# A hybrid decoder layer on one core: first weights on ScalarE's queue, and last additions ahead of the preceding scalings

## The chip, the core and the metric

The kernel runs on one core of a Trainium2 chip. A core has five engines with an instruction queue each. TensorE (PE in the profile) multiplies matrices; PEld is its loading of the stationary operand. VectorE (DVE) and ScalarE (ACT) work on tiles elementwise, GpSimd (POOL) too, and SyncE (SP) mostly issues DMAs. A DMA is an instruction on the queue of the engine that issues it, and its data are moved by 16 DMA engines that all queues share. An engine executes its queue in order, and an instruction that waits for a semaphore holds up everything behind it.

The metric is the device time of one execution, in microseconds (us). Less is better.

## The reference, cut to what matters

One pre-norm layer: a root-mean-square norm of 16 meta tokens and 512 tokens of width 2048, one combined input projection, three causal token mixers on its columns, a gate on each branch, one output projection with a residual add, and a final norm.

```python
def hybrid_layer(x, norm_w, w_in, ...):
    h = rms_norm(x, norm_w)
    ...
    proj = (h @ w_in).astype(f32)
    (dq, dk, dv, dz, db, da, gq, gk, gv, gz, gl, fq, fk, fv, fz, ff) = split_cols(proj)
    ...
    o_dn = gated_head_norm(o_dn, dz, ...)          # gated delta rule, 6 heads
    o_gla = gated_head_norm(o_gla, gz, ...)        # gated linear attention, 5 heads
    o_fox = o_fox.reshape(fz.shape) * jax.nn.silu(fz)   # forgetting attention, 5 heads
    o = jnp.concatenate([o_dn, o_gla, o_fox], axis=-1)
    return x + o @ w_out

def reference(x, meta_tokens, ...):
    h = jnp.concatenate([meta, x], axis=1)
    h = hybrid_layer(h, ...)
    return rms_norm(h, final_norm_w)[:, N_META:]
```

All of it is float32. The kernel keeps that accuracy on TensorE by writing each operand as a sum of two parts, hi and lo, and adding three products: hi by hi, hi by lo, and lo by hi.

## The kernel before

**Scheduling.** The program is written with a tile framework. A scheduler orders each engine's queue with a simulated timeline of its own, by priorities and by the dependencies that it is given. The kernel adds dependencies that cost no semaphore ("NoSync": they only fix an order on one engine); `paced`, `behind` and `ring` are such. DMAs from SP and ACT take one of eight completion semaphores in turn (order shows them as DMAHW0 to DMAHW7), and a DMA that takes a semaphore again waits until the DMA that held it before has landed.

**The start.** The norm's weight is folded into the transposed input. For a 128-row block k of the width, `load_x` makes `xh{k}` (ACT, scaled copy of the raw block `xs`, line 302) and `xl{k}` (DVE, the rest, line 303). Two blocks come in one tile: `xs0` holds blocks 0 and 1, and is loaded as two DMAs (line 287); `xs1` to `xs7` are one DMA each (line 280). Tokens are scaled by their norm only after the projection, so a second copy of the input in token order, `xt00` to `xt41` (line 349, 512 KB each for tokens, less for meta tokens), is squared and summed on ACT (line 350).

The first four column blocks of the projection (gates `dz` of heads 0 to 3, `NF = 4`) are computed together, because their four sums can use the same input blocks as they come. Their weights come in quarters of the depth: `raw{i}q{q}` is quarter q of weight i, 256 KB (line 186). A weight is split by `split`: `pace[0]` is ACT's copy to hi (line 170), `pace[1]` DVE's subtraction that gives lo (line 171). A quarter of depth has 4 blocks, 4 weights and 3 products, 48 matmuls of 512 columns (line 314, sums `pp0`, `pp1`, `pp2`, `pp12` in the order of the queue). While TensorE waits for the first data, it multiplies a tile of ones, ten times (`warm`, line 309), and once more behind the first three real matmuls (line 335).

Other loads of the start are 8 KB of constants on ACT's queue (`cpk`, columns 0 to 15, line 126: the norm weight that `xh` and `xl` need), the remaining 42.5 KB of constants (line 136) and a mask `lm` (line 137), which `more_constants` reads on DVE as `dnws` and `lmk` (lines 139 and 138).

**The middle.** Every other block of the input projection follows with 1024-column loads, split in the same way; the mixers' smaller work is placed between their matmuls. The output projection uses sums and differences of weight blocks that GpSimd's accumulating DMAs build. None of it is touched.

**The end.** The output is computed for four token blocks `tb` of 128 and four column groups `cc` of 512. For the last group, `cc` 3, TensorE finishes the token blocks one after the other (`pt30`, `pt31`, `pt32`, `pt33` with 384 columns, and `pz` with the last 128). For each token block DVE adds TensorE's sum to the accumulator that holds the residual (`add`, line 1429, tiles `acc` and `accs`), ACT squares and sums (`square`, line 1436), DVE makes the mean (lines 1601 and 1602; 1597 and 1598 for the last block), ACT takes logarithm and exponential to get the reciprocal root `r` (lines 1608 and 1609), and the four groups are scaled by it: groups 0 and 2 on ACT (line 1613), group 1 on DVE (line 1617), group 3 on DVE together with the final norm's weight (line 1615). Each group then goes out by DMA (line 1618). For the last token block the 384 columns are squared on ACT and the last 128 by one DVE instruction (line 1605). GpSimd multiplies groups 0 to 2 by the final norm's weight beforehand (`weigh`, line 1439).

Of the kernel before, what the change touches and what calls it, by code (L numbers as in the profile page):

```python
# [8 lines left out]
F32 = mybir.dt.float32  # L9
F32R = mybir.dt.float32r  # L10
# [3 lines left out]
AF = mybir.ActivationFunctionType  # L14
ALU = mybir.AluOpType
# [3 lines left out]
P = 128  # L19
D = 2048  # L20
# [6 lines left out]
EPS = 1e-6  # L27
# [15 lines left out]
def _cols():  # L43

    def run(start, n):
        return list(range(start, start + n))

    none = lambda n: [-1] * n
    gates = run(5004, 16) + run(5004, 16) + run(3072, 6) + run(3078, 6) + run(7580, 5) + none(15)
    blocks, name = [], {}  # L50

    def add(key, cols):
        name[key] = len(blocks)
        blocks.append(cols)

    for g in range(2):
        for h in range(H * g, H * g + H):
            add(("dz", h), run(2304 + P * h, P))
        for what, start in (("dk", 768), ("dv", 1536), ("dq", 0)):
            for h in range(H * g, H * g + H):  # L60
                add((what, h), run(start + P * h, P))
    for h in range(GLA_HEADS):
        add(("gz", h), run(4364 + P * h, P))
    for p in range(3):
        if p < 2:
            add(("gk", p), run(3404 + P * p, P))
            add(("gq", p), run(3084 + P * p, P))
        else:
            add(("gk", p), run(3404 + P * p, 64) + run(3084 + P * p, 64))
        for h in range(2 * p, min(2 * p + 2, GLA_HEADS)):  # L70
            add(("gv", h), run(3724 + P * h, P))
    for h in range(FOX_HEADS):
        for what, start in (("fk", 5660), ("fv", 6300), ("fq", 5020), ("fz", 6940)):
            add((what, h), run(start + P * h, P))
    return gates, [c for b in blocks for c in b], name


GATE_COLS, COLS, BLOCK_OF = _cols()
# [4 lines left out]
def tile_hybrid_trunk(ctx, tc, xT, xtok, mtok, w_gate, w_in, w_out, w_dn, consts, lmask, fin_w, out, dbg=None):  # L83
    nc = tc.nc
# [6 lines left out]
    six = pool("six", 14)  # L91
# [5 lines left out]
    def row(name, dt=F32):  # L97
        return wk.tile([P, 3 + T], dt, tag="row", bufs=7, name=name)
# [4 lines left out]
    V, A, G, PE = nc.vector, nc.scalar, nc.gpsimd, nc.tensor  # L103
# [20 lines left out]
    nwc, cwc = cpk[:, 0:16], cpk[:, 16:88].rearrange("p (b w) -> p b w", w=4)  # L124
# [43 lines left out]
    def split(raw, hi, lo):  # L168
        with tc.high_priority(offset=1000000):
            pace[0] = A.copy(hi, raw).ins  # L170
            pace[1] = V.tensor_tensor(out=lo, in0=raw, in1=hi.bitcast(F32), op=ALU.subtract).ins  # L171
            splits.append(pace[1])
            heads_.append(pace[0])
# [3 lines left out]
    def paced(*ins):  # L177

        for x in ins:
            tc.add_manual_dep(x.ins, pace[x.ins.engine == pace[1].engine].name, mybir.DependencyInfo(  # L180
                mybir.DependencyClass.NoSync, mybir.DependencyReason.DATA), reason="paced")

    def raw_rows(src, name):

        raw = row(f"raw{name}")[:, : src.shape[-1]]
        nc.sync.dma_start(out=raw, in_=src)
        return raw, name

    def split_rows(raw, name):

        n = raw.shape[-1]
        both = six.tile([P, 2, 512], F32R, tag="six", name=f"w{name}")
        hi, lo = both[:, 0, :n], both[:, 1, :n]
        split(raw, hi, lo)
        return hi, lo


    def part(name, n=512):
        return hp.tile([P, T], F32R, tag="x", name=name)[:, :n]
# [37 lines left out]
    xh, xl = [], []  # L237
# [32 lines left out]
    NF = 4  # L270

    def first_quarter(i, q):
        return raw_rows(w_in[BLOCK_OF["dz", i], q // 2][:, (q % 2) * 512 : (q % 2 + 1) * 512], f"{i}q{q}")

    xs = {}

    def fetch_x(c):
        xs[c] = six.tile([P, 2, T], F32, tag="six", name=f"xs{c}")
        if c > 0:
            nc.sync.dma_start(out=xs[c], in_=xT[:, 2 * c : 2 * c + 2, :])  # L280

    firsts = []

    def fetch_first():
        fetch_x(0)
        for j in range(2):
            nc.sync.dma_start(out=xs[0][:, j], in_=xT[:, j])
            firsts.append(first_quarter(j, 0))
        firsts.extend(first_quarter(i, 0) for i in (2, 3))
        fetch_x(1)  # L290

    def load_x(c):
        if c not in xs:
            fetch_x(c)
        t = xs[c]
        for j in range(2):
            k = 2 * c + j
            if c == 0 and j == 1:
                wq.append(split_rows(*firsts[0]))
            xh.append(part(f"xh{k}", T))  # L300
            xl.append(part(f"xl{k}", T))
            A.activation(xh[k], t[:, j], AF.Copy, scale=nwc[:, k : k + 1])
            V.scalar_tensor_tensor(out=xl[k], in0=t[:, j], scalar=nwc[:, k : k + 1],
                                   in1=xh[k].bitcast(F32), op0=ALU.mult, op1=ALU.subtract)


    pw = psm.tile([P, 512], F32, tag="m", name="warm")
# [12 lines left out]
    for q in range(4):  # L320
        wq = []
# [22 lines left out]
    for b in range(5):  # L344
        r = NM if b == 4 else P
        for c in range(2):
            t = wp.tile([P, 1024], F32, tag=("raw", "hi", "lo")[(2 * b + c) % 3], name=f"xt{b}{c}")
            src = mtok if b == 4 else xtok[b * P : (b + 1) * P]
# [6 lines left out]
    for b in range(5):  # L355
        r = NM if b == 4 else P
# [85 lines left out]
    raw = row("rawgk")[:48, :320]  # L442
# [193 lines left out]
    raw = {}  # L636
# [771 lines left out]
    def mms(p_, o, w, s, first, last):  # L1408
        for n, (o_, w_) in enumerate(((o[0], w[0]), (o[0], w[1]), (o[1], w[0]))):
            mm = PE.matmul(p_, o_[:, s], w_, start=(first and n == 0), stop=(last and n == 2), skip_group_check=True)  # L1410
            order.append(mm.ins)
# [15 lines left out]
    def add(tb, cc, p_, c=slice(0, 512), op=ALU.add):  # L1427
        a = acc[tb, cc][:, c]
        return V.tensor_tensor(out=a, in0=a, in1=p_[:, c], op=op)
# [4 lines left out]
    def square(tb, cc, c=slice(0, 512), n=0):  # L1434
        sq = row(f"sqf{tb}{cc}{n}")
        A.activation(sq[:, c], acc[tb, cc][:, c], AF.Square, accum_out=ss[:, tb, cc + n : cc + n + 1])

    def weigh(tb, cc):
        return G.tensor_tensor(out=acc[tb, cc], in0=acc[tb, cc], in1=fw[cc], op=ALU.mult)  # L1439
# [45 lines left out]
    for j in pairs:  # L1485
        r = raw[j]
        paced(V.scalar_tensor_tensor(out=r["a12"], in0=r["a12"], scalar=-1.0, in1=r["s2"], op0=ALU.mult,
                                     op1=ALU.subtract))
        r["s4"] = r["a12"]
    for mm, n in later:  # L1490
        n = head[n[0]] + n[1] if isinstance(n, tuple) else n
# [66 lines left out]
    fw, marks = [], []  # L1558
    for c in range(4):
        f = part(f"fw{c}").bitcast(F32)  # L1560
# [16 lines left out]
    for cc in range(3):  # L1577
        for tb in range(4):
            x = weigh(tb, cc)
            tc.add_manual_dep(x.ins, marks[1 if cc == 0 and tb < 3 else 2].name, mybir.DependencyInfo(  # L1580
                mybir.DependencyClass.Sync, mybir.DependencyReason.DATA), reason="paced")
    if LAST:
        add(3, 3, pa[3], slice(CUT, 512))
    for tb in range(4):
        cuts = 2 if tb == 3 else 1
        for n in range(cuts):
            c = slice(0, 512) if cuts == 1 else slice(CUT, 512) if n else slice(0, CUT)
            p_ = psm.tile([P, 512], F32, tag="m", name="pz") if n else pa[tb]
            for i in range(LAST, NP):
                mms(p_[:, c], oparts[i], [t[:, c] for t in wl[i]], slice(tb * P, (tb + 1) * P),  # L1590
                    (n == 1 or LAST == 0) and i == LAST, i == NP - 1)
            add(tb, 3, p_, c)
            if n < 1:
                square(tb, 3, c, n)
                if tb == 3:
                    r = rr[:, tb : tb + 1]
                    V.reduce_sum(r, ss[:, tb, :4], axis=mybir.AxisListType.X)
                    V.tensor_scalar(r, r, 1.0 / D, EPS, ALU.mult, ALU.add)
        r = rr[:, tb : tb + 1]
        if tb < 3:  # L1600
            V.reduce_sum(r, ss[:, tb, :4], axis=mybir.AxisListType.X)
            V.tensor_scalar(r, r, 1.0 / D, EPS, ALU.mult, ALU.add)
        else:
            a = acc[tb, 3][:, c]
            V.tensor_tensor_reduce(out=row("sqz")[:, c], in0=a, in1=a, scale=1.0 / D, scalar=r, op0=ALU.mult,
                                   op1=ALU.add, accum_out=rr[:, 4:5])
            r = rr[:, 4:5]
        A.activation(r, r, AF.Ln)
        A.activation(r, r, AF.Exp, scale=-0.5)
        for cc in (1, 0, 3, 2):  # L1610
            a = acc[tb, cc]
            if cc % 2 == 0:
                A.activation(a, a, AF.Copy, scale=r)
            elif cc == 3:
                V.scalar_tensor_tensor(out=a, in0=a, scalar=r, in1=fw[cc], op0=ALU.mult, op1=ALU.mult)
            else:
                V.tensor_scalar_mul(a, a, r)
            (nc.scalar if tb == 3 and cc == 2 else nc.sync).dma_start(
                out=out[tb * P : (tb + 1) * P, cc * 512 : (cc + 1) * 512], in_=a)

# [59 lines left out]
```

## Time and profile before

| | us |
|---|---|
| median of 3 runs | 987.03 |
| lowest and highest run | 986.32, 987.07 |
| the profiled execution, its time | 986.87 |
| the profiled execution, its span (first to last instruction) | 985.2 |
| TensorE busy in that span | 975.0 (99%) |
| VectorE busy | 670.5 (68%) |
| ScalarE busy | 480.3 (49%) |

Rows of the profile name a line, an engine, an operation and its tiles. In rows in order of time the first number is the start in us from the span's start, the second the duration; what stands in brackets is the idle time of the engine ahead of the row and who ended it. A tile's number is left out there, so `xh` is any of `xh0` to `xh15`, and `w0q` the hi or the lo part of weight 0.

### The profile page before, as it was taken

Reading aid. Unit: us, or ns where it says so; the run is one execution under the profiler, and the core shown is the slowest. Engines: PE = TensorE matmul, PEld = TensorE weight load, DVE = VectorE, ACT = ScalarE, POOL = GpSimd, SP = SyncE. Lnnn points to the kernel's source line nnn. Section 1 sums busy time; section 2 is a strip of 40 time slices with the busy share of each in tenths; the row PEclk is TensorE's granted clock in tenths of the full one; section 3 lists DMA queues with packets and bytes.
Section 4 is the critical chain, followed back from the end, with each engine's and each line's share of the span. In section 5 each row is a group of like instructions: output and inputs, shape, how many; then the busy total and the mean of one; then the engine's idle time right before and its main releaser. Section 6 shows DMA issues by size and latency. Waiting matters only on the chain.

```text
span 985.2 us, 19830 instructions
## 1 busy us (share of the span) xinstructions
PE 975.0 (99%) x7762; PEld 894.4 (91%) x7762; DVE 670.5 (68%) x1462; ACT 480.3 (49%) x1051; POOL 218.2 (22%) x237
## 2 busy tenths in 40 slices
PE   9999999999999999999999999999999999999996
PEld 7899999899999888899899988899999998888885
DVE  5457886975657985334685847867767768987665
ACT  7753534344456334234546445655555545644345
POOL 0021322222123334201213122333322120000033
PEclk9999999999999999999999999999999999999998
DMA  9835598887458787644646666677766588366534
GB/s 345 303 119 206 161 251 222 238 257 224 127 164 221 212 252 191 164 112 102 154 138 161 158 153 194 190 218 218 195 200 171 174 267 296 132 214 212 186 115 172
DMA packets 70339, 191.83 MB, mean 195 GB/s; under 512 B 14077, under 2 KB 17325, under 8 KB 69476
## 3 DMA queue, kind: packets, MB, share of 16 engines
q1 hardware_dynamic: 46048, 152.53, 45.2%
q0 software_dynamic: 15104, 31.66, 18.4%
q10 hardware_dynamic: 9092, 6.36, 2.4%
q8 instruction: 61, 1.00, 0.4%
q14 instruction: 34, 0.28, 0.1%
HBM read 179.84 MB, written 60.88 MB: 244 GB/s over the span
## 4 chain that ended last, share of the span: by engine, by line
PE 98%; DVE 1%; ACT 1%; issue 0%; POOL 0%; DVEq 0%; ACTq 0%; POOLq 0%
PE pp L245 49%; PE pp_a L580 8%; PE pq L1410 6%; PE pp L314 5%; PE pa L1410 3%; PE ps L1410 3%; PE pt L1410 2%; PE pp_b L580 2%; PE pp_d L580 2%; PE pp_c L580 2%; PE pr L1410 1%; PE pss L1059 1%; PE pgate L431 1%; PE pfo L1285 1%; PE pfa L1237 1%; PE pg L723 1%
## 5 line engine op out<-in xcount | busy, mean ns | idle before, releaser
L245 PE MATMUL pp<-xl,whi 128*128 128x264 f32 (+2 forms) x1120 | 273.9, 306 | 0.0
L245 PE MATMUL pp<-xh,whi 128*128 128x264 f32 (+2 forms) x1120 | 272.9, 306 | 0.0
L245 PE MATMUL pp<-xh,wlo 128*128 128x264 f32 (+2 forms) x1120 | 272.2, 305 | 0.0
L170 ACT CAST whi<-raw 128x1024 fp32r<-128x1024 f32 x131 | 137.2, 1047 | 180.2 <-PE pp L245 125.1
L171 DVE TENSOR_TENSOR wlo<-raw,whi 128x1024 fp32r<-128x1024 f32 x131 | 162.8, 1243 | 66.4 <-ACT whi L170 56.0
L245 PEld LDWEIGHTS pp<-xl,whi 128*128 128x128 f32 x1120 | 182.7, 189 | 9.1 <-issue 0.4
L245 PEld LDWEIGHTS pp<-xh,whi 128*128 128x128 f32 x1120 | 182.3, 189 | 9.2 <-issue 0.2
L245 PEld LDWEIGHTS pp<-xh,wlo 128*128 128x128 f32 x1120 | 182.8, 189 | 8.5 <-issue 0.2
L390 POOL TENSOR_SCALAR stc<-cv 128x528 f32<-128x528 f32 (+1 forms) x18 | 28.1, 1563 | 145.8 <-DVE cv L622 136.2
L622 DVE SCALAR_TENSOR_TENSOR cv<-pb,cpk,cv 128x528 f32<-128x528 f32 (+1 forms) x54 | 41.1, 760 | 0.8
L1439 POOL TENSOR_TENSOR acc<-acc,fw 128x512 f32<-128x512 f32 x4 | 6.1, 1542 | 138.9 <-DVE wll L171 138.9
L170 ACT CAST whis<-raws 128x1024 fp32r<-128x1024 f32 x20 | 20.7, 1049 | 28.0 <-PE ps L1410 9.7
L171 DVE TENSOR_TENSOR wlos<-raws,whis 128x1024 fp32r<-128x1024 f32 x20 | 24.2, 1222 | 14.8 <-ACT whis L170 14.8
L580 PE MATMUL pp_a<-t,whi 128*128 128x264 f32 (+1 forms) x224 | 30.3, 283 | 0.0
L580 PEld LDWEIGHTS pp_a<-t,whi 128*128 128x128 f32 x224 | 28.0, 188 | 0.4
L580 PE MATMUL pp_a<-xh,whi 128*128 128x264 f32 x112 | 28.1, 286 | 0.0
L580 PE MATMUL pp_a<-xl,whi 128*128 128x264 f32 x112 | 27.9, 285 | 0.0
L379 DVE TENSOR_TENSOR pb<-pp,rstd 128x264 f32<-128x264 f32 (+1 forms) x36 | 13.8, 421 | 17.3 <-PE pp L245 17.3
L1410 PE MATMUL pq<-whia,a 128*128 128x512 f32 x80 | 25.4, 393 | 0.0
L1410 PE MATMUL ps<-whis,s 128*128 128x512 f32 x80 | 25.4, 394 | 0.0
L1410 PE MATMUL pq<-whis,s 128*128 128x512 f32 x80 | 25.4, 394 | 0.0
L390 POOL TENSOR_SCALAR stdz<-zdz 128x512 f32<-128x512 f32 x6 | 11.2, 1877 | 63.2 <-DVE zdz L408 62.2
(506 smaller groups left out, 2111.4 us busy)
## 6 DMA issues: line engine op xcount, KB each, us to landing
raw<-in_w_in SPq DMA_DIRECT2D x103, 512.0 KB, 3.6
ti<-in_w_in SPq DMA_DIRECT2D x28, 512.0 KB, 5.3
raw<-ti SPq DMA_DIRECT2D x28, 512.0 KB, 3.7
tw<-in_w_dn SPq DMA_DIRECT2D x20, 512.0 KB, 5.2
raws<-tw SPq DMA_DIRECT2D x15, 512.0 KB, 4.3
ti<-in_w_in POOLq DMA_DIRECT2D x14, 512.0 KB, 6.0
ti<-ti POOLq DMA_DIRECT2D x14, 512.0 KB, 7.0
tw<-in_w_dn POOLq DMA_DIRECT2D x10, 512.0 KB, 6.9
```

Source lines behind the costliest of these rows:

```text
L170: pace[0] = A.copy(hi, raw).ins
L171: pace[1] = V.tensor_tensor(out=lo, in0=raw, in1=hi.bitcast(F32), op=ALU.subtract).ins
L245: mm = PE.matmul(p_[:, :nt], wt[:, j * m : (j + 1) * m], xx[k][:, t0 : t0 + nt], start=(k == 0 and wt is hi and xx is xh), stop=(k == KT - ...
L314: mm = PE.matmul(ps[:, :S], wt[:, j * P : (j + 1) * P], xx[k][:, NM:T], start=(k == 0 and wt is hi and xx is xh), stop=(k == KT - 1 and wt ...
L379: V.tensor_tensor(out=o, in0=p_[rows], in1=rstd[rows, t0 : t0 + n], op=ALU.mult)
L390: maxes.append(G.tensor_scalar_max(t, src, LOW).ins)
L431: PE.matmul(pgate[a][:, :HT], wg[k // 8][:, k % 8, :], xx[k][:, a * HT : (a + 1) * HT], start=(k == 0 and xx is xh), stop=(k == KT - 1 and ...
L580: m = PE.matmul(p_[:, cols], wt[:, j * P : (j + 1) * P], xx[j][part_][:, cols], start=first and i == 0, stop=i == len(todo) - 1, skip_grou ...
L622: V.scalar_tensor_tensor(out=c, in0=pb[:, t0 + w : w + T], scalar=cwc[:, blk, w : w + 1], in1=c, op0=ALU.mult, op1=ALU.add)
L723: PE.matmul(pg[:r, j * r : (j + 1) * r], kT[:, j, ts], kT[:, j, ts], start=True, stop=True)
L1059: mm = PE.matmul(ps[o0 : o0 + n, b * n : b * n + n], kx[rr, k0 : k0 + n], qx[rr, q0 : q0 + n], start=True, stop=True)
L1410: mm = PE.matmul(p_, o_[:, s], w_, start=(first and n == 0), stop=(last and n == 2), skip_group_check=True)
```

## The change

Two places are edited.

At the start, the first quarter of the four weights is issued from ACT's queue instead of SP's. The first of them is no longer split by `split`, but by a new function, `split_first`, with both parts on DVE: a copy and the subtraction. The `paced` call fixes that the input block 2 (first of `xs1`) follows the splitting of the weights on ACT and DVE.

At the end, a NoSync dependency puts each token block's addition for group 3 ahead of the preceding block's two DVE scalings in DVE's queue; for the last block, the addition of the last 128 columns is put behind the first 384 columns' mean.

```diff
-    def raw_rows(src, name):
+    def raw_rows(src, name, queue=None):
 
         raw = row(f"raw{name}")[:, : src.shape[-1]]
-        nc.sync.dma_start(out=raw, in_=src)
+        (queue or nc.sync).dma_start(out=raw, in_=src)
         return raw, name
...
     def first_quarter(i, q):
-        return raw_rows(w_in[BLOCK_OF["dz", i], q // 2][:, (q % 2) * 512 : (q % 2 + 1) * 512], f"{i}q{q}")
+        return raw_rows(w_in[BLOCK_OF["dz", i], q // 2][:, (q % 2) * 512 : (q % 2 + 1) * 512], f"{i}q{q}",
+                        None if q else nc.scalar)
+
+    def split_first(raw, name):
+
+        both = six.tile([P, 2, 512], F32R, tag="six", name=f"w{name}")
+        hi, lo = both[:, 0], both[:, 1]
+        V.tensor_copy(hi, raw)
+        V.tensor_tensor(out=lo, in0=raw, in1=hi.bitcast(F32), op=ALU.subtract)
+        return hi, lo
...
             if c == 0 and j == 1:
-                wq.append(split_rows(*firsts[0]))
+                wq.append(split_first(*firsts[0]))
...
-            A.activation(xh[k], t[:, j], AF.Copy, scale=nwc[:, k : k + 1])
-            V.scalar_tensor_tensor(out=xl[k], in0=t[:, j], scalar=nwc[:, k : k + 1],
-                                   in1=xh[k].bitcast(F32), op0=ALU.mult, op1=ALU.subtract)
+            x = A.activation(xh[k], t[:, j], AF.Copy, scale=nwc[:, k : k + 1])
+            y = V.scalar_tensor_tensor(out=xl[k], in0=t[:, j], scalar=nwc[:, k : k + 1],
+                                       in1=xh[k].bitcast(F32), op0=ALU.mult, op1=ALU.subtract)
+            if c == 1 and j == 0:
+                paced(x, y)
...
+    scaled = []
     for tb in range(4):
...
-            add(tb, 3, p_, c)
+            x = add(tb, 3, p_, c).ins
+            for y in scaled if n < 1 else [r]:
+                tc.add_manual_dep(*((y, x.name) if n < 1 else (x, y.name)), mybir.DependencyInfo(
+                    mybir.DependencyClass.NoSync, mybir.DependencyReason.DATA), reason="behind")
+            scaled = []
...
-                    V.tensor_scalar(r, r, 1.0 / D, EPS, ALU.mult, ALU.add)
+                    r = V.tensor_scalar(r, r, 1.0 / D, EPS, ALU.mult, ALU.add).ins
...
             elif cc == 3:
-                V.scalar_tensor_tensor(out=a, in0=a, scalar=r, in1=fw[cc], op0=ALU.mult, op1=ALU.mult)
+                scaled.append(V.scalar_tensor_tensor(out=a, in0=a, scalar=r, in1=fw[cc], op0=ALU.mult,
+                                                     op1=ALU.mult).ins)
             else:
-                V.tensor_scalar_mul(a, a, r)
+                scaled.append(V.tensor_scalar_mul(a, a, r).ins)
```

Because the scheduler decides the rest, other instructions of the start move too. SP's queue shows the loads of the start. Before, from the second weight on (`xs1` and `xs2` are input blocks 2 to 5, `cpk` the remaining constants):

```order
L186 DMA raw1q0_119<-in_w_in 128x512
L186 DMA raw2q0_121<-in_w_in 128x512
L186 DMA raw3q0_123<-in_w_in 128x512
L280 DMA xs1_125<-in_xT 128x1056
L186 DMA raw0q1_218<-in_w_in 128x512
L186 DMA raw1q1_223<-in_w_in 128x512
L186 DMA raw2q1_238<-in_w_in 128x512
L186 DMA raw3q1_243<-in_w_in 128x512
L136 DMA cpk_94<-in_consts 128x85
L280 DMA xs2_208<-in_xT 128x1056
```

After, from the start of SP's queue:

```order
L296 DMA xs0_114<-in_xT 128x528 x2
L289 DMA xs1_125<-in_xT 128x1056
L136 DMA cpk_94<-in_consts 128x85
L137 DMA lm32_296<-in_lmask 128x192
L186 DMA raw0q1_218<-in_w_in 128x512
L186 DMA raw1q1_223<-in_w_in 128x512
L186 DMA raw2q1_238<-in_w_in 128x512
L186 DMA raw3q1_243<-in_w_in 128x512
L360 DMA xt00_480<-in_xtok 128x1024
L360 DMA xt01_483<-in_xtok 128x1024
L360 DMA xt10_486<-in_xtok 128x1024
L289 DMA xs2_208<-in_xT 128x1056
```

The four weights have left it for ACT's queue, the constants and the mask stand ahead of the second quarter's weights, and three token-order tiles stand ahead of `xs2`. On ACT their three squarings stand ahead of `xh4` likewise.

DVE's queue at the start, before:

```order
L303 SCALAR_TENSOR_TENSOR xl0_132<-xs0_114,cpk_94,xh0_131 128x528
L171 TENSOR_TENSOR w0q0_135<-raw0q0_116,w0q0_135 128x512
L303 SCALAR_TENSOR_TENSOR xl1_139<-xs0_114,cpk_94,xh1_138 128x528
L171 TENSOR_TENSOR w1q0_142<-raw1q0_119,w1q0_142 128x512
L171 TENSOR_TENSOR w2q0_145<-raw2q0_121,w2q0_145 128x512
L171 TENSOR_TENSOR w3q0_148<-raw3q0_123,w3q0_148 128x512
```

and after:

```order
L280 CAST w0q0_135<-raw0q0_116 128x512
L281 TENSOR_TENSOR w0q0_135<-raw0q0_116,w0q0_135 128x512
L312 SCALAR_TENSOR_TENSOR xl0_132<-xs0_114,cpk_94,xh0_131 128x528
L139 TENSOR_SCALAR dnws_101<-cpk_94 128x1
L312 SCALAR_TENSOR_TENSOR xl1_139<-xs0_114,cpk_94,xh1_138 128x528
L171 TENSOR_TENSOR w1q0_142<-raw1q0_119,w1q0_142 128x512
L138 CAST lmk_100<-lm32_296 128x192
L171 TENSOR_TENSOR w2q0_145<-raw2q0_121,w2q0_145 128x512
L171 TENSOR_TENSOR w3q0_148<-raw3q0_123,w3q0_148 128x512
```

`dnws`, which reads the remaining constants, now stands ahead of `xl1`, and `lmk`, which reads the mask, ahead of the lo part of weight 2; before, both stood among the second quarter's rows.

DVE's queue at the end, from the second token block's scalings on (`frs` is the mean and then the reciprocal root, `accs` tiles are the accumulators, `fw3` the final norm's weight), before:

```order
L1617 TENSOR_SCALAR accs4_10223<-accs4_10223,frs_10051 128x512
L1615 SCALAR_TENSOR_TENSOR accs13_10442<-accs13_10442,frs_10051,fw3_11122 128x512
L1429 TENSOR_TENSOR accs13_10442<-accs13_10442,pt32_11294 128x512
L1601 TENSOR_REDUCE frs_10051<-fss_10050 128x1
L1602 TENSOR_SCALAR frs_10051<-frs_10051 128x1
L1617 TENSOR_SCALAR accs4_10223<-accs4_10223,frs_10051 128x512
L1615 SCALAR_TENSOR_TENSOR accs13_10442<-accs13_10442,frs_10051,fw3_11122 128x512
L1429 TENSOR_TENSOR accs13_10442<-accs13_10442,pt33_11295 128x384
L1429 TENSOR_TENSOR accs13_10442<-accs13_10442,pz_11430 128x128
L1597 TENSOR_REDUCE frs_10051<-fss_10050 128x1
L1598 TENSOR_SCALAR frs_10051<-frs_10051 128x1
```

and after:

```order
L1440 TENSOR_TENSOR accs13_10442<-accs13_10442,pt32_11294 128x512
L1634 TENSOR_SCALAR accs4_10223<-accs4_10223,frs_10051 128x512
L1631 SCALAR_TENSOR_TENSOR accs13_10442<-accs13_10442,frs_10051,fw3_11122 128x512
L1617 TENSOR_REDUCE frs_10051<-fss_10050 128x1
L1618 TENSOR_SCALAR frs_10051<-frs_10051 128x1
L1440 TENSOR_TENSOR accs13_10442<-accs13_10442,pt33_11295 128x384
L1634 TENSOR_SCALAR accs4_10223<-accs4_10223,frs_10051 128x512
L1631 SCALAR_TENSOR_TENSOR accs13_10442<-accs13_10442,frs_10051,fw3_11122 128x512
L1613 TENSOR_REDUCE frs_10051<-fss_10050 128x1
L1614 TENSOR_SCALAR frs_10051<-frs_10051 128x1
L1440 TENSOR_TENSOR accs13_10442<-accs13_10442,pz_11430 128x128
```

Each addition now precedes the scalings of the block before it, and the last 128 columns' addition follows the last mean. TensorE's order changes only among the matmuls of the start (weight 3's first ones go behind weight 2's and among those of block 2, and two small ones for the norm come some 30 rows earlier), and GpSimd's not at all.

## Prediction

> **What bounds the kernel now.** The page's first part comes first, for where the time can be at all.
>
> ```profile
> span 985.2 us, 19830 instructions
> ...
> PE 975.0 (99%) x7762; PEld 894.4 (91%) x7762; DVE 670.5 (68%) x1462; ACT 480.3 (49%) x1051; POOL 218.2 (22%) x237
> ```
>
> TensorE is busy for 975.0 of 985.2 us. Of the 10.2 us that are left, 8.4 follow its last matmul (976.80, below), so 1.8 remain for the start and everything between. The time is what passes before TensorE runs without gaps, then a fixed amount of matmuls, then what follows the last of them. The change touches the first and the third; a shift of TensorE at the start goes through to the end undiminished, since there is next to no wait behind it that could swallow it.
>
> The start, in order of time: ScalarE, then a row of VectorE, then three of TensorE:
>
> ```profile
> 3.94 0.73 ACT L302 ACTIVATE xh<-xs,cpk 128x528 fp32r<-128x528 f32 x1 [1.87 <-DMA cpk<-in_consts]
> 4.58 0.60 ACT L170 CAST w0q<-raw0q 128x512 fp32r<-128x512 f32 x1
> 6.11 0.74 ACT L302 ACTIVATE xh<-xs,cpk 128x528 fp32r<-128x528 f32 x1 [0.92 <-DMA xs<-in_xT]
> 6.75 0.62 ACT L170 CAST w1q<-raw1q 128x512 fp32r<-128x512 f32 x1
> 7.41 0.62 ACT L170 CAST w2q<-raw2q 128x512 fp32r<-128x512 f32 x1
> ...
> 13.81 0.74 ACT L302 ACTIVATE xh<-xs,cpk 128x528 fp32r<-128x528 f32 x1 [0.42 <-DMA xs<-in_xT]
> ```
> ```profile
> 13.64 0.15 DVE L139 TENSOR_SCALAR dnws<-cpk 128x1 f32<-128x1 f32 x1
> ```
> ```profile
> 5.48 0.77 PE L314 MATMUL pp<-xh,w0q 128*128 128x512 f32 x1
> ...
> 7.99 0.39 PE L314 MATMUL pp<-xl,w0q 128*128 128x512 f32 x1
> ...
> 17.71 0.40 PE L314 MATMUL pp<-xh,w0q 128*128 128x512 f32 x1
> ```
>
> ScalarE follows the landings: w2 comes 0.66 us after w1, which is 256 KB at about 400 GB/s. TensorE's first real matmul is at 5.48; its seventh, the one of `xl1`, at 7.99. At 17.71 starts the first one of `xh4`, which is the 49th (a quarter has 48): 42 matmuls in 9.72 us, 0.23 each, without a gap. Had they run so from 5.48, the seventh had been at 5.48 + 6 x 0.23 = 6.9. So 1.1 us is all that could be won at the start. The DMA engines in that time:
>
> ```profile
> 4.00:5.00 1.00, 1.00 (x7) 1.00 (x7) 0.29 (x1) 1.00 (x2) 0.00 (x0) 1.00 1.02 306
> 6.00:7.00 1.00, 1.00 (x6) 0.74 (x4) 0.20 (x2) 0.89 (x2) 0.00 (x0) 1.00 0.83 234
> 12.00:14.00 2.00, 2.00 (x10) 1.61 (x9) 2.00 (x5) 1.56 (x5) 0.00 (x0) 1.00 1.05 405
> ```
>
> The last two numbers of a row are the engines' busy share and GB/s: nearly full all along. The start is bound by bytes, and their order decides what comes when. Against 405 GB/s the first two rows lack 0.24 and 0.42 us, 0.67 together.
>
> **The change at the start.** ScalarE's queue now brings w0 to w3 while SP's brings `xs0` (two DMAs), `xs1`, the remaining constants, the mask. I take it that the engines serve both queues in turn, packet by packet. Then:
> - w0 lands together with the second half of `xs0`. The same bytes had landed before at 6.11; without the 1.5 us that this half took behind w0, at 4.58 + 0.66 = 5.24. Before, w0 was there at 4.58.
> - w1 shares with `xs1`: together 768 KB, three times 0.66, so at 7.2 to 8.1, before 6.75.
> - The remaining constants stand behind `xs1` and share with w2: 0.7 to 0.75 later, at 7.9 to 8.8. They had been needed only at 13.64.
> - w3 shares with the mask, 8.9 to 9.8; `xh2` stands behind its cast as before, and is needed late.
>
> VectorE's copy of w0 isn't in the trace. Bounds: 0.15 (the one-column row above) to 0.67 (an addition of two tiles of that shape, in a row below); I take 0.49, a scaling of that shape, below too, which like a copy reads one tile. ScalarE loses the 0.60 cast, and gains four DMA issues; the fourth, w3's, takes the constants' semaphore and so waits for them at about 3.9, with `xh0` behind it for some 0.4: hidden, since w0 comes later than 4.4. VectorE: copy and subtraction of w0, `xl0` (0.77), free at 6.9 to 7.8. Then `dnws` waits for the constants until 7.9 to 8.8, 0.15, and `xl1` behind it, 0.7, is ready at 8.75 to 9.65. That is the seventh matmul, 7.99 before: **+0.8 to +1.65**. With the engines' missing 0.67 us made good as well it is +0.1. So even then nothing is gained. Weights 2 and 3 are behind `xl1` in TensorE's order and come in time.
>
> A second bound: `xs2` now stands behind three token-order tiles of 512 KB and the mask, 1.67 MB more, 4.1 us at 405 GB/s: it lands at 17.9 and not at 13.81; `xh4` follows after 0.74 at 18.65, against 17.71: +0.95. With the 0.67 us made good it is +0.3. This bound isn't added; the later one counts. For the start I take **+1.3**, between 0.95 and 1.65.
>
> The rule that speaks against this change is in the Trainium skill, "DMA: Bandwidth & Descriptors", section "Issuing engines are not separate DMA queues": DMAs of several engines run on the same 16 DMA engines and interleave, and issuing from two engines saves only issue time. The trace agrees so far: busy shares of 1.02 and 0.83 above with SP's queue nearly alone. By that rule the sum is the one made here; by its opposite, w1 to w3 landing beside the inputs at no cost, 1.1 us would be saved at the start.
>
> **The change at the end**, in rows of VectorE, ScalarE, TensorE and GpSimd:
>
> ```profile
> 967.89 1.79 DVE L1615 SCALAR_TENSOR_TENSOR accs<-accs,frs,fw 128x512 f32<-128x512 f32 x1
> 969.61 0.67 DVE L1429 TENSOR_TENSOR accs<-accs,pt 128x512 f32<-128x512 f32 x1
> 971.07 0.16 DVE L1601 TENSOR_REDUCE frs<-fss 128x1 f32<-128x4 f32 x1 [0.79 <-ACT sqf L1436]
> 971.99 0.49 DVE L1617 TENSOR_SCALAR accs<-accs,frs 128x512 f32<-128x512 f32 x1 [0.58 <-ACT frs L1609]
> 972.39 0.75 DVE L1615 SCALAR_TENSOR_TENSOR accs<-accs,frs,fw 128x512 f32<-128x512 f32 x1
> 973.06 0.68 DVE L1429 TENSOR_TENSOR accs<-accs,pt 128x512 f32<-128x512 f32 x1
> ...
> 976.51 0.55 DVE L1429 TENSOR_TENSOR accs<-accs,pt 128x384 f32<-128x384 f32 x1
> 976.98 0.28 DVE L1429 TENSOR_TENSOR accs<-accs,pz 128x128 f32<-128x128 f32 x1
> 977.74 0.16 DVE L1597 TENSOR_REDUCE frs<-fss 128x1 f32<-128x4 f32 x1 [0.48 <-ACT sqf L1436]
> 978.12 0.35 DVE L1605 CUSTOM_DVE_ANT_0 sqz<-accs,frs 128x128 f32<-128x128 f32 x1
> ```
> ```profile
> 976.01 0.71 ACT L1613 ACTIVATE accs<-accs,frs 128x512 f32<-128x512 f32 x1
> 977.10 0.52 ACT L1436 ACTIVATE sqf<-accs 128x384 f32<-128x384 f32 x1 [0.38 <-DVE accs L1429]
> ```
> ```profile
> 971.29 0.40 PE L1410 MATMUL pt<-wlh,ol 128*128 128x512 f32 x1
> ...
> 974.51 0.34 PE L1410 MATMUL pt<-wlh,ol 128*128 128x384 f32 x1
> ...
> 976.53 0.27 PE L1410 MATMUL pz<-wlh,ol 128*128 128x128 f32 x1
> ```
> ```profile
> 961.37 7.77 POOL L1439 TENSOR_TENSOR accs<-accs,fw 128x512 f32<-128x512 f32 x6
> ```
>
> TensorE ends block 2 at 971.69, the 384 columns at 974.85, all at 976.80, but VectorE adds at 973.06, 976.51, 976.98: 1.4 and 1.7 us late, behind scalings. The last addition costs nothing by itself; the mean after it waits until 977.74 for ScalarE's square, which waited for the addition at 976.51. After, on the same clock: block 1's sum is there at 967.6 (18 matmuls of 0.23 before 971.69), added by 968.2; block 0's scalings follow, and the second, which took 1.79 until GpSimd was done at 969.14, ends at 969.8, hardly later than the 969.68 before, so the addition falls into a time that was lost anyway. Block 1's mean at 969.8 (before 971.07); VectorE then waits for TensorE until 971.69, adds by 972.35, scales block 1 by 973.4 (0.36 late, which nobody waits for); block 2's mean at 973.4; the 384 columns added from 974.87 to 975.4; block 2's scalings until 976.4 (before 976.51); meanwhile ScalarE, whose two scalings of block 2 end at 975.6 (some 0.5 after the mean for the root, then 0.7 each), squares by 976.25, not 977.7. The last mean is done at 976.78, the last addition runs 976.82 to 977.1, and the square-and-sum starts at 977.13 and not at 978.12: **-1.0**. From there on everything, the four last DMAs too, is the same chain 1.0 earlier. The mean ends 0.02 ahead of TensorE, so a slip anywhere takes from the gain: bounds 0 and -1.05; I take -0.95.
>
> **The sum.** +1.3 - 0.95 = +0.35. On the profiled execution's 986.87 it is 987.2, on the median 987.03, **987.4**. About 0.2% (2 us) is what a measurement of this kernel can tell from no change; the forecast is within it.
>
> **The rivals.** *Slower, by TensorE's clock.* The loading of a 128x128 operand shows it:
>
> ```profile
> 5.63 0.33 PEld L314 LDWEIGHTS pp<-xl,w0q 128*128 128x128 f32 x1
> 6.89 0.19 PEld L314 LDWEIGHTS pp<-xh,w0q 128*128 128x128 f32 x1
> ```
>
> It falls from 0.33 to 0.19 after some 5 us of unbroken matmuls from 1.2 on. Now the `warm` matmuls end at about 5.4 as before, but w0 isn't there until 5.7 to 6.6, and only six real matmuls run until 9. If that breaks the run-up, it starts anew at about 9: 5 us at a speed of 0.19/0.33, so 2.1 us lost, and the start costs 3.4: 989.5. It decides if TensorE does less than half its work between 5.4 and 9. For it: the gap. Against: most of the run-up is over by 5.4. "TensorE: Matmul & The Clock Gate" of the Trainium skill, "Part 1", has the full clock after about 3.4 us of sustained work and lost after an idle window of as much; by its window, an estimate, 1.4 us would be lost.
>
> *A little faster: the engines fill their gaps.* With two queues the 234 and 306 GB/s become 400; the start is then bound at +0.3 by `xs2`, and the sum is 986.4. For it: busy shares under 1 at 6 to 7 us. Against: 306 GB/s at a share of 1.02.
>
> *The end gives nothing.* If additions that wait for TensorE hold up scalings that ScalarE or the DMAs need, the end stays: 988.3. Against: the walk above, in which the late scaling has no follower.
>
> *The start does what it is for*: 1.1 us won, 985.0. Against: the constants ahead of `xl1`.
>
> **Chances.** Forecast 0.58, clock 0.12, filled gaps 0.20, end without gain 0.07, start won 0.03. Slower by over 0.2% (over 989.0): the clock's 0.12. Faster (under 985.1): 0.03. Same: 0.85. The range of 986.0 to 989.0 leaves out the start won, most of the clock, and little of the filled gaps.
>
> **What would show it.** Right: `xl1` on VectorE behind a wait for the constants' DMA, TensorE's seventh matmul at 8.8 to 9.7, a wait for `xh4` only if the start is early; VectorE's additions directly behind TensorE at the end, and 7.4 us from TensorE's last matmul to the end of the span in place of 8.4. Wrong: a seventh matmul before 8, loading at 0.33 beyond 7 us, or a last mean that still waits for ScalarE.

## The result, and the profile after

The changed kernel takes 989.28 us (median of 10 runs, 988.48 to 990.77), the kernel before 987.06 (986.32 to 988.08) beside it. The ratio is 1.0024, with a 95% interval of 1.0014 to 1.0033: slower, by 2.2 us where +0.35 was forecast, and 0.3 us above the range. The profiled execution took 988.94 us, against 986.87 before.

```profile
span 987.2 us, 19825 instructions
...
PE 976.4 (99%) x7762; PEld 894.9 (91%) x7762; DVE 668.3 (68%) x1463; ACT 479.5 (49%) x1050; POOL 218.2 (22%) x237
```

The number of matmuls is the same, yet TensorE is busy 1.4 us longer: some of its matmuls have become slower. First the start, in the order of time: four rows of ScalarE, five of VectorE, eight of TensorE.

```profile
4.35 0.74 ACT L311 ACTIVATE xh<-xs,cpk 128x528 fp32r<-128x528 f32 x1 [2.27 <-DMA cpk<-in_consts]
5.50 0.73 ACT L311 ACTIVATE xh<-xs,cpk 128x528 fp32r<-128x528 f32 x1 [0.42 <-DMA xs<-in_xT]
7.99 0.62 ACT L170 CAST w1q<-raw1q 128x512 fp32r<-128x512 f32 x1 [1.75 <-DMA raw1q<-in_w_in]
...
18.90 0.74 ACT L311 ACTIVATE xh<-xs,cpk 128x528 fp32r<-128x528 f32 x1
```
```profile
5.95 0.43 DVE L280 CAST w0q<-raw0q 128x512 fp32r<-128x512 f32 x1 [5.95 <-DMA raw0q<-in_w_in]
6.41 0.69 DVE L281 TENSOR_TENSOR w0q<-raw0q,w0q 128x512 fp32r<-128x512 f32 x1
7.02 0.76 DVE L312 SCALAR_TENSOR_TENSOR xl<-xs,cpk,xh 128x528 fp32r<-128x528 f32 x1
8.60 0.15 DVE L139 TENSOR_SCALAR dnws<-cpk 128x1 f32<-128x1 f32 x1 [0.82 <-DMA cpk<-in_consts]
8.68 0.77 DVE L312 SCALAR_TENSOR_TENSOR xl<-xs,cpk,xh 128x528 fp32r<-128x528 f32 x1
```
```profile
6.52 0.47 PE L325 MATMUL pp<-xh,w0q 128*128 128x512 f32 x1 [0.96 <-DVE w0q L280]
7.83 0.50 PE L325 MATMUL pp<-xl,w0q 128*128 128x512 f32 x1 [0.85 <-DVE xl L312]
...
9.12 0.63 PE L325 MATMUL pp<-xh,w1q 128*128 128x512 f32 x1
9.55 0.63 PE L325 MATMUL pp<-xl,w1q 128*128 128x512 f32 x1
9.97 0.63 PE L325 MATMUL pp<-xl,w0q 128*128 128x512 f32 x1
10.40 0.63 PE L325 MATMUL pp<-xh,w0q 128*128 128x512 f32 x1
...
12.52 0.40 PE L325 MATMUL pp<-xh,w1q 128*128 128x512 f32 x1
...
20.63 0.40 PE L325 MATMUL pp<-xh,w0q 128*128 128x512 f32 x1
```

w0 is there at 5.95, w1 at 7.99, the constants at 8.60. From 9.12 on TensorE waits for nothing, but its matmuls start 0.43 us apart, and by 12.5 us 0.23 apart again. The stretches view (the columns after the engines' busy times are the granted clock, the DMA engines' busy share and GB/s) shows why:

```profile
5.15:8.56 3.41, 1.60 (x10) 1.04 (x8) 1.80 (x3) 1.31 (x2) 0.00 (x0) 1.00 1.04 394
8.56:11.97 3.41, 3.41 (x11) 2.74 (x10) 3.37 (x7) 3.06 (x7) 0.00 (x0) 0.50 0.98 299
```

In the 3.41 us up to 8.56 TensorE was busy for 1.60, 47%; then for exactly as long its clock was halved. The first matmul of `xh4` stands at 20.63 (17.71 before), 2.92 late, though `xh4` was ready at 18.90 + 0.74 = 19.64. The lateness then stays as it is to the end, where VectorE's last rows and TensorE's last read:

```profile
977.84 0.56 DVE L1440 TENSOR_TENSOR accs<-accs,pt 128x384 f32<-128x384 f32 x1 [1.15 <-PE pt L1421]
978.31 0.48 DVE L1634 TENSOR_SCALAR accs<-accs,frs 128x512 f32<-128x512 f32 x1
978.71 0.75 DVE L1631 SCALAR_TENSOR_TENSOR accs<-accs,frs,fw 128x512 f32<-128x512 f32 x1
979.37 0.15 DVE L1613 TENSOR_REDUCE frs<-fss 128x1 f32<-128x4 f32 x1
...
979.80 0.29 DVE L1440 TENSOR_TENSOR accs<-accs,pz 128x128 f32<-128x128 f32 x1
980.12 0.35 DVE L1621 CUSTOM_DVE_ANT_0 sqz<-accs,frs 128x128 f32<-128x128 f32 x1
```
```profile
979.49 0.28 PE L1421 MATMUL pz<-wlh,ol 128*128 128x128 f32 x1
```

The additions now wait for TensorE and not for scalings; the last one starts 0.03 after TensorE's end (979.77), the square-and-sum 0.35 after it, where it had been 1.32. The chain behind it keeps this gain of 0.97 up to the last scaling (979.46 before, 981.46 after), and 0.07 of it is lost behind that: from TensorE's end to the span's it is 7.46 us (979.77 to 987.23), 8.36 before (976.80 to 985.16). So TensorE ends 2.97 us later and the end is 0.90 shorter: +2.07 in the span, as in the time of the profiled execution.

### The profile page after: what moved, and what is told of

It is laid out like the page before. It is cut to its first block, busy times and chain, and to the rows that moved or that the text cites. A ratio compares the mean times of both kernels' runs of the same rounds, so it can differ in the third digit from the quotient of the medians.

```text
span 987.2 us, 19825 instructions
## 1 busy us (share of the span) xinstructions
PE 976.4 (99%) x7762; PEld 894.9 (91%) x7762; DVE 668.3 (68%) x1463; ACT 479.5 (49%) x1050; POOL 218.2 (22%) x237
## 4 chain that ended last, share of the span: by engine, by line
PE 98%; DVE 1%; DMA 0%; issue 0%; ACT 0%
PE pp L245 49%; PE pp_a L591 8%; PE pq L1421 6%; PE pp L325 5%; PE pa L1421 3%; PE pt L1421 3%; PE ps L1421 3%; PE pp_b L591 2%; PE pp_d L591 2%; PE pp_c L591 2%; PE pr L1421 1%; PE pss L1070 1%; PE pgate L442 1%; PE pfo L1296 1%; PE pfa L1248 1%; PE pg L734 1%
```

## The experiments

Each set of four ran on one chip, beside runs of the kernel before on that chip. There the kernel before spread over 3 to 4 us, so medians within 1 us of each other say little, and most verdicts rest on the traces. The table collects what is read from them. "Late" is how much later a matmul starts than the same one in the trace of before: the 40th real one (at 15.6 us there, ahead of `xh4`), the 60th (20.3) and the 300th (64.2). "Half" says if the clock was halved at the start. "Tail" is the time from TensorE's end to the span's. The last two columns are the median less that of the kernel before beside it, and the ratio with its interval.

| run | late, 40th | 60th | 300th | half | tail | median, us | ratio |
|---|---|---|---|---|---|---|---|
| changed kernel | 2.91 | 2.91 | 2.91 | yes | 7.5 | +2.2 | 1.0014 to 1.0033 |
| e5 changed, again | 3.33 | 3.33 | 3.46 | yes | 7.5 | +3.2 | 1.0022 to 1.0047 |
| e1 end only | 0.12 | 0.12 | 0.12 | no | 7.4 | -1.2 | 0.9984 to 1.0001 |
| e12 end only, again | 0.18 | 0.18 | 0.18 | no | 7.5 | -0.5 | 0.9992 to 1.0010 |
| e2 start only | 3.03 | 3.03 | 3.67 | yes | 8.2 | +3.1 | 1.0020 to 1.0045 |
| e3 idle filled | 2.11 | 2.90 | 3.61 | no | 7.6 | +2.3 | 1.0014 to 1.0033 |
| e4 before, fewer warm-ups | 0.41 | 0.41 | 0.42 | no | 9.1 | +0.8 | 1.0000 to 1.0018 |
| e6 all loads on SyncE | 0.22 | 0.22 | 0.22 | no | 7.5 | -0.5 | 0.9990 to 1.0007 |
| e7 tiles held | 3.03 | 3.03 | 3.06 | yes | 7.5 | +2.0 | 1.0014 to 1.0032 |
| e8 held, filled | 4.25 | 4.25 | 4.26 | yes | 7.6 | +1.7 | 1.0010 to 1.0028 |
| e9 held, filled more | 2.09 | 2.09 | 2.11 | no | 7.6 | +1.2 | 1.0000 to 1.0018 |
| e10 no wait for constants | 1.84 | 1.84 | 1.85 | no | 7.4 | +0.2 | 0.9994 to 1.0012 |
| e11 only w0 on ScalarE | 0.47 | 0.47 | 0.55 | no | 7.5 | +0.1 | 0.9991 to 1.0008 |

### Which half of the change costs the time

The theory after the first look (A) was that the clock decides. e1 is the changed kernel with this undone, e2 the changed kernel with only this kept:

```diff
-        (queue or nc.sync).dma_start(out=raw, in_=src)
+        nc.sync.dma_start(out=raw, in_=src)
...
-                wq.append(split_first(*firsts[0]))
+                wq.append(split_rows(*firsts[0]))
...
-            if c == 1 and j == 0:
-                paced(x, y)
```

> The start of the kernel before with the end of the changed one. Theory A (the changed kernel's +2.25 us is a start 2.96 us later, of which 1.3 us is data that lands later and 1.65 us a TensorE at half its clock for 3.4 us, and an end 0.96 us shorter): the end is worth the same by itself, TensorE's last matmul at 976.8 as before, the span 7.4 us longer than that, 986.1 us in all. Rival (the shorter end in the changed kernel is owed to its later start, say to output DMAs or GpSimd that lie elsewhere): less than 0.5 us, 986.6 to 987.0. In neither case slower than before.

> The start of the changed kernel with the end of the one before. Theory A: TensorE's last matmul at 979.7 and 8.4 us behind it, 990.0 to 990.3 us, 0.95 us above the changed kernel; granted clock 0.5 from about 8.6 to 11.9 us again. Rival (start and end are not independent): 989.3 or less.

Measured: 986.32 and 990.67 us, against 987.55 for the kernel before. The two halves are independent: e1 has the start of before and the short tail, e2 the late start and a tail of 8.2. All of the loss is in the start. e12 repeats e1 on another chip:

> The kernel before with the end of the changed one, a second time, for the interval: 0.96 us below the kernel before, ratio 0.9990, 7.4 us behind the last matmul where the kernel before has 8.4. Rival (the end's gain is lost again somewhere the profile doesn't show): ratio 1.000.

The median is 986.72 against 987.19. The tail is 7.47 us, but neither interval of the two separates the time from no change, and that of e12, from 0.9992 on, just leaves out the 0.9990 that was expected. The shorter end is shown by every trace that has it, eleven with 7.4 to 7.6 us against 8.2 to 9.1 in the three that don't, and by no verdict of the times.

### Is it the clock

e3 fills TensorE's two idle stretches in the changed kernel; e4 takes warm-up matmuls away from the kernel before (10 to 7 in the first loop there):

```diff
-    for i in range(10):
+    for i in range(12):
         PE.matmul(pw[:, :P], ones, ones, start=True, stop=True)
...
+            if k == 0 and wt is hi and xx is xh and ps is begun[0][0][0]:
+                with tc.issue_after(mm.ins):
+                    for _ in range(3):
+                        PE.matmul(pw[:, :P], ones, ones, start=True, stop=True)
```

> The changed kernel with both idle stretches of TensorE at the start (5.57 to 6.52, 6.99 to 7.83 us) filled by matmuls on constants that nothing reads: twelve instead of ten ahead of the first real matmul, three more behind it. No load, no copy, no wait is changed. Theory A: the granted clock stays at 1.0 through 8 to 12 us, the seventh real matmul starts at about 9.4 us when xl1 is ready and not at 9.97, TensorE's last matmul comes 1.5 us earlier, 987.6 to 987.8 us in all. Rival B (the halved clock is a by-product, and weights and inputs that land late hold TensorE back by 2.96 us in any case): 989.3 us as the changed kernel, with waits for w1, w2, w3 or xl1 in place of slow matmuls.

> The kernel before with seven warm-up matmuls instead of ten, so that TensorE is idle for some 1.2 us ahead of its first real matmul at 5.48 us; nothing else is touched. Theory A: the clock is not up by 6.3 us, or falls again later; a stretch of 3.4 us at half the clock costs 1.0 to 1.7 us: 988.0 to 988.8 us. Rival B: the idle time costs nothing, since the first real matmul starts no earlier or later than before: 987.1 us.

Theory A did not hold. e3 kept its clock, as it was to, and took 989.80 us all the same, +2.3. In its TensorE rows waits stand in place of the slow matmuls:

```profile
9.13 0.50 PE L325 MATMUL pp<-xh,w1q 128*128 128x512 f32 x1 [0.36 <-ACT w1q L170]
...
20.53 0.50 PE L325 MATMUL pp<-xh,w0q 128*128 128x512 f32 x1 [0.55 <-ACT xh L311]
...
37.88 0.50 PE L325 MATMUL pp<-xh,w0q 128*128 128x512 f32 x1 [0.44 <-ACT xh L311]
```

The first is the late w1, the second `xh4`, the third `xh10`: 2.1 us late, then 2.9, then 3.6. And e4 did not lose its clock, with TensorE idle for 1.0 us ahead of its first real matmul; so it says how much idle time the clock bears, and nothing of what a lost clock costs. The 3.41 us in which that lies, and the ones of e8 (below) in which the clock was lost:

```profile
4.42:7.83 3.41, 2.33 (x10) 1.65 (x10) 2.67 (x4) 2.30 (x4) 0.00 (x0) 1.00 0.94 292
```
```profile
6.09:9.50 3.41, 1.85 (x12) 1.41 (x12) 1.88 (x5) 0.70 (x2) 0.00 (x0) 1.00 1.05 389
9.50:12.92 3.42, 3.42 (x11) 2.75 (x10) 3.42 (x8) 3.11 (x7) 0.00 (x0) 0.50 0.88 256
```

Busy for 2.33 of 3.41 the clock stays, for 1.85 it goes.

### Three bounds on top of each other

The new theory (N): the halved clock, `xh4` and `xh10` each hold TensorE back about as far, so taking one away shows the next. e5 is the changed kernel unaltered. e6 puts all first loads back on SyncE's queue (`None` in place of `nc.scalar`) and keeps the rest. e7 puts the token-order tiles behind `xs2`, `xs3`, `xs4` and `xs5`; e8 is e7 and e3 at once.

```diff
-            nc.sync.dma_start(out=t[:r], in_=src[:, c * 1024 : (c + 1) * 1024])
+            d = nc.sync.dma_start(out=t[:r], in_=src[:, c * 1024 : (c + 1) * 1024])
+            tc.add_manual_dep(d.ins, xdma[min(2 * b + c + 2, 5)].ins.name, mybir.DependencyInfo(
+                mybir.DependencyClass.NoSync, mybir.DependencyReason.DATA), reason="behind")
```

> The changed kernel unaltered, beside the three others of this set. Theory N (three bounds lie nearly on top of each other at the start: a TensorE at half its clock, +2.9 us by 12 us; xh4, whose input stands behind three token-order tiles, +2 to +2.9 us; xh10, whose input stands behind four more, up to +3.6 us): 1.9 to 2.9 us above the kernel before, whether or not this execution loses the clock. Theory A (the clock decides): about 2 us above it where the clock is lost, 0.5 where it isn't.

> The changed kernel with all first loads on SyncE's queue as before; the split of w0 on VectorE and the end stay. Theory N: the whole loss is in the queue and what it does to the order of the loads, so the start is that of the kernel before to within 0.4 us, no wait for xh4 or xh10, 7.4 us from the last matmul to the end of the span: 0.6 to 1.2 us below the kernel before. Rival (VectorE's copy and subtraction of w0 cost the start by themselves): TensorE's first real matmul or the seventh is 0.5 us or more later than before, and the time within 0.5 us of the kernel before.

> The changed kernel with the token-order tiles put behind xs2, xs3, xs4 and xs5 on SyncE's queue and so on ScalarE; the two queues, the split and the idle stretches of TensorE are left. Theory N: no wait for xh4 or xh10; the clock may still fall, then TensorE's last matmul is 2.9 us later than in the kernel before and the time 1.9 us above it; where it doesn't fall, the seventh matmul's delay alone is left, 1.4 to 2.1 us, and the time is 0.5 to 1.1 us above. Theory A: the same as the changed kernel, 2 us above.

> Both at once: token-order tiles held back as in the run above, and TensorE's idle stretches filled with matmuls that nothing reads. Theory N: with clock and late inputs both out of the way what is left is the seventh matmul, 1.4 to 2.1 us late (w1's cast and xl1); with the end's 0.96 us that is 0.5 to 1.1 us above the kernel before, and 1.0 to 1.8 us under the changed one, where filling alone gave nothing. Rival (the inputs land late because the DMA engines move only some 240 GB/s from 10 to 13.5 us, whatever stands first): a wait for xh4 or the weights of the second quarter remains, and the time is 1.5 us or more above the kernel before.

Medians: 990.35, 986.71, 989.20 and 988.94 us, against 987.20. e6 settles the part: with the loads back on one queue the start is 0.22 us late and no more, so the second queue costs nearly all, and VectorE's copy and subtraction of w0 hardly anything. In e7 no later matmul waits for `xh4` or `xh10`, and the start is 3.03 late all the same. Most of that is the first quarter's data and not the clock: in this execution w1 landed only at 9.14 and the constants at 9.76, so that `xl1` was ready at 9.84 + 0.77 = 10.61, 2.62 behind the 7.99 at which its matmul had started before. That leaves the clock 0.4 us at most. e8 missed its purpose: w0 landed at 7.3 us in that execution, the twelve warm-ups were over at 6.5, and the clock was lost again. A row of VectorE in e7, one of TensorE in e8:

```profile
9.84 0.77 DVE L312 SCALAR_TENSOR_TENSOR xl<-xs,cpk,xh 128x528 fp32r<-128x528 f32 x1
```
```profile
7.85 0.47 PE L325 MATMUL pp<-xh,w0q 128*128 128x512 f32 x1 [1.39 <-DVE w0q L280]
```

In e5, the changed kernel again, and in e2, with the same start, the late inputs hide the clock. A row of ScalarE in e5 (`xh4`), one of TensorE in e2 (`xh10`):

```profile
20.17 0.74 ACT L311 ACTIVATE xh<-xs,cpk 128x528 fp32r<-128x528 f32 x1
```
```profile
37.94 0.50 PE L325 MATMUL pp<-xh,w0q 128*128 128x512 f32 x1 [0.36 <-ACT xh L311]
```

In e5 `xh4` is ready at 20.91, 3.20 behind the 17.71 of before, where TensorE is 3.33 late: the clock adds 0.1 us. In e2 TensorE, 3.03 late up to there, still waits for `xh10`, and is 3.67 late behind it, as it is in e3 with a full clock (3.61).

e9 is e8 with fifteen warm-ups. e10 is e9 with the two VectorE instructions on the constants and the mask ordered behind `xl3` (the same kind of order-only dependency). e11 is the changed kernel with `nc.scalar` for w0 alone.

> The run with token-order tiles held back and idle stretches filled, with fifteen warm-up matmuls instead of twelve, so that TensorE stays busy until w0 is there even where w0 lands at 7.3 us as it did in that run. Theory N: the clock stays at 1.0, no input is waited for from the second quarter on, and what is left at the start is the later landing of w0, w1 and the constants: TensorE 1.4 to 2.1 us late from the seventh matmul on, 0.5 to 1.1 us above the kernel before. Rival (the inputs come 2.9 us late in any case): TensorE's hundredth matmul is again 2.9 us or more late, 2 us above the kernel before.

> As e9_held_warm15, and the two VectorE instructions on the late constants and the mask put behind xl3, so that xl1 waits for neither. If the prediction's first term is right (xl1 stands behind a wait for the constants, and this sets the seventh matmul), TensorE is 0.5 to 0.9 us earlier than in e9_held_warm15: 0.6 to 1.4 us late. If w1 decides instead (its cast starts when it lands, at 8.0 to 8.6 us), it is at most 0.3 us earlier.

> The changed kernel with only w0 on ScalarE's queue, w1 to w3 on SyncE's as before. Bytes decide: w0 and the two halves of xs0 land together at 5.2 to 5.9 us, w1 and all behind it as before; the token-order tiles stand where they stood in the kernel before. TensorE starts 0.2 to 0.9 us late and has it nearly made good by w2: shift 0 to 0.5 us, and with the end 0.5 to 1.0 us below the kernel before. Rival (any second queue brings the order of the loads and the clock down): 1.5 us or more above it.

Medians: 988.41, 987.40 and 987.33 us, against 987.19. e9 is as theory N has it: clock kept, no later wait, 2.1 us late. What remains are the loads of the first quarter, in the rows of TensorE and of VectorE:

```profile
9.11 0.50 PE L325 MATMUL pp<-xh,w1q 128*128 128x512 f32 x1 [0.42 <-ACT w1q L170]
...
9.98 0.50 PE L325 MATMUL pp<-xl,w0q 128*128 128x512 f32 x1
```
```profile
9.08 0.15 DVE L139 TENSOR_SCALAR dnws<-cpk 128x1 f32<-128x1 f32 x1 [1.64 <-DMA cpk<-in_consts]
9.15 0.77 DVE L312 SCALAR_TENSOR_TENSOR xl<-xs,cpk,xh 128x528 fp32r<-128x528 f32 x1
```

Without the wait for the constants (e10) it is 1.84 us: the wait is worth 0.25, and w1, which lands at 8.4 to 8.6 in these two and not at 6.75, the rest. e11, with w1 back on SyncE's queue behind `xs0`, is 0.47 late, with the clock kept; its time differs from that of the kernel before by no more than the runs can tell. No kernel of the study was shown to beat the kernel before. e1, e6 and e12, all first loads on one queue as before and the new end, come nearest, with medians 0.5 to 1.2 us under it and intervals that take in 1.000.

## Why the prediction was wrong

**What bounds the kernel: right.** The shift at the start went to the end undiminished: 2.91 at the 300th matmul, 2.97 at TensorE's end.

**The first landings: right in this execution, towards the late end.** w0 5.95 (5.24 to 6.1 forecast), w1 7.99 (7.2 to 8.1), the constants 8.60 (7.9 to 8.8), `xl1` ready at 9.45 (8.75 to 9.65). The copy took 0.43 us for an estimated 0.49. That the bounds held was in part luck: in the seven other traces with all four weights on ScalarE's queue w1 came at 8.4 to 9.1 and the constants at 9.1 to 9.8, later than any time that was forecast. The rule of the Trainium skill that was set against the change ("DMA: Bandwidth & Descriptors", section "Issuing engines are not separate DMA queues") holds here: e6 differs from the changed kernel in the queue alone, and the order that follows from it, and runs 3.1 us ahead of it (0.22 against 3.33 late on the same chip). **That `xl1` behind the constants sets the seventh matmul** was only a quarter us of it; w1's later landing would have done nearly the same.

**The start's size, +1.3 from a bound of 0.95 to 1.65: wrong, and the first of the two steps that failed.** In the changed kernel's own profile the term that was mis-sized is that of `xh4`. `xl1`, ready at 9.45, was 1.46 behind the 7.99 of its matmul before and so within its bounds; `xh4` was ready at 19.64 against 17.71, +1.93, where +0.95 stood. `xs2` was there not at 17.9 but at 18.9, when `xh4` starts. The 405 GB/s of before, on which that rested, weren't there:

```profile
10.00:12.00 2.00, 2.00 (x6) 1.62 (x5) 2.00 (x5) 2.00 (x4) 0.00 (x0) 0.51 0.93 240
12.00:14.00 2.00, 2.00 (x10) 1.62 (x10) 2.00 (x5) 1.68 (x4) 0.00 (x0) 1.00 0.97 297
```

Against 405 these four us lack (405 - 240) x 2 + (405 - 297) x 2 = 546 KB, 1.35 us of transfers. The step "with the engines' missing 0.67 us made good" had looked only for an improvement. `xh10`, behind four more tiles, wasn't priced at all. Its row in the changed kernel (ScalarE), and its first matmul in the kernel before:

```profile
35.65 0.72 ACT L311 ACTIVATE xh<-xs,cpk 128x528 fp32r<-128x528 f32 x1
```
```profile
34.39 0.40 PE L314 MATMUL pp<-xh,w0q 128*128 128x512 f32 x1
```

It is ready at 36.37, +1.98, and is the latest of the bounds in e2 and e3. The first term has a size of its own in other executions: in e9, with the clock kept and later inputs out of the way, the first quarter alone is 2.1 late, since w1 came at 8.44 and the constants at 9.08 there, past the bounds of 8.1 and 8.8, which had been made from the landing rate of one execution.

**The clock, a rival at 0.12: wrong, the second step that failed.** The argument against it, that the run-up was over by 5.4, doesn't matter: a full clock is lost again. The point given for it to decide, less than half of TensorE's work between 5.4 and 9, was met with 47% in the 3.41 us up to 8.56. The sign that was given for it came too, a loading at 0.33 beyond 7 us, and it moved the seventh matmul to 9.97, past the 8.8 to 9.7 of the forecast:

```profile
9.12 0.33 PEld L325 LDWEIGHTS pp<-xl,w1q 128*128 128x128 f32 x1
```

In the changed kernel's profile the halved clock costs 2.92 - 1.93, about 1.0 us, and not the 2.1 that the rival gave, since `xh4` would have held TensorE at +1.93 without it. So the sum for this execution should have been about +2.0 for `xh4` and `xh10`, +0.9 to 1.0 for the clock, -0.9 for the end: +2.0 to +2.1, where the spans differ by 2.07. In e5 and e2 the clock was lost too, but cost 0.1 us or nothing, since `xh4` was 3.2 us late in e5 and `xh10` 3.5 in e2. So in the three traces of this start the late inputs make up most of the loss, and the clock between nothing and 1.0 us of it. The rival's 989.5 was near the time by luck, with terms that were not: its clock too large, its landings too small.

**The end, -0.95: right, step by step.** Square-and-sum 0.33 us after TensorE's last matmul forecast, 0.35 measured; the mean done 0.02 ahead of TensorE forecast, its reduction at 979.37 and so well ahead of 979.77 measured; 7.4 us to the end of the span forecast, 7.46 measured; -0.90 in all. That the delayed scalings have no follower holds to within the 0.07 us lost behind the last of them.

**The rivals:** engines that fill their gaps ran the other way from 10 us on; the start that wins 1.1 us is excluded by the landings; an end that gives nothing, by the tails.

## What to carry to other kernels

Where a start is bound by bytes, a second queue mostly reorders them: ask which load stands first in line for every later consumer, and price all the bounds that come out, since the second and third may lie within a us of the first. Late data can cost twice if TensorE goes idle for it and its clock is halved: look at its busy share over the 3.4 us up to each gap, not at the gap alone. Of two bounds that overlap, removing one may show nothing; remove both before concluding that neither counts. And bounds that are made from one execution's landings are too narrow where another execution lands up to 1.1 us later, as w1 did here.

## What the runs showed of the hardware

The clock. In five traces (the changed kernel, e2, e5, e7, e8) it was halved after a stretch of 3.41 us with TensorE busy for 1.43 to 1.85 us of it (42% to 54%), for the next 3.41 us; it stayed full where TensorE was busy for 2.33 (68%) or more. Where the stretches lie differs from run to run: the halved one began at 8.56 us in the changed kernel's profile and at 9.50 in e8's. The Trainium skill ("TensorE: Matmul & The Clock Gate", section "Part 1: The HAM clock gate (the "warmup" mystery)") has a window of 3413 ns that runs freely, which agrees. It has the clock fall after an idle window; here a half-busy one was enough, with no gap longer than 1.4 us.

From 10 to 12 us the DMA engines moved 240 to 281 GB/s in seven of the eight traces with four loads on ScalarE's queue (240 in the changed kernel, 281 in e9 and e5), at busy shares of 0.81 to 0.98, so the packets took longer. In the kernel before it was 402 at that time, and 409 in e6. In e10, the eighth, it was 360, so that four loads on a second queue don't always bring it down. What slows the engines wasn't found: it isn't the halved clock, since e3 and e9 have the low rate with a full one.

One execution can differ from another by some 2 us at one place in the middle, at about 560 us, where TensorE's small matmuls into `pss` wait for their operands. The waits of TensorE in e6 show it:

```profile
PE pss L1070 <- ACT kq L1079: 1.3, 1, 1.3
...
PE pss L1070 <- DVE kq L1056: 0.8, 1, 0.8
```

In the profile of before neither of these waits is there. Why they come and go was not tried. They may be a part of the spread of 3 to 4 us between runs of the kernel before; of those runs only one was profiled, so that is not shown.
